# Recurrent mixer: where the casts to the matmul format run, and the low part of the mixed output

## The chip, the cores and the metric

The kernel runs on one core of one Trainium2 chip. The metric is the device time of one execution in microseconds, the median over several runs. The core has a matrix engine (TensorE; PE in the profile, its weight loads PEld), three engines for elementwise work (VectorE is DVE, ScalarE is ACT, GpSimd is POOL) and a queue engine for loads (SyncE, SP). Each engine runs its own instructions strictly in the order in which they stand in its queue; between engines, semaphores hold an instruction until its data are there.

## The reference

A trunk of two layers on 512 tokens of width 1024. Layer 0 has a convolution mixer, layer 1 a recurrent mixer; behind each stands a mixture of 16 experts. The change lies in the recurrent mixer of layer 1:

```python
u = jnp.einsum("bsd,de->bse", x, w_in)
y_branch, xr = jnp.split(u, 2, axis=-1)
xr = causal_depthwise_conv(xr, c_dw) + c_dw_b
...
r = jax.nn.sigmoid(jnp.einsum("bshi,hij->bshj", xh, w_gate_a) + b_gate_a)
i = jax.nn.sigmoid(jnp.einsum("bshi,hij->bshj", xh, w_gate_x) + b_gate_x)
...
a = jnp.exp(log_a)
mult = jnp.sqrt(-jnp.expm1(2.0 * log_a))
b = mult * (i * xr).astype(jnp.float32)
_, h = lax.associative_scan(_linear_recurrence_combine, (a, b), axis=1)
out = jax.nn.gelu(y_branch) * h.astype(x.dtype)
return jnp.einsum("bse,ed->bsd", out, w_out)
```

## The kernel before, in words

Every matrix product that must hold float32 precision is made of three products: each operand is split into a high part (the value cast to the matmul format fp32r) and a low part (the value minus the high part). `hilo` does this for activations: the cast on ScalarE (`act=True`) or on VectorE (`act=False`), the subtraction always on VectorE. The same is done for weights in `Stream`: the cast on ScalarE (L137), the subtraction (L148) on VectorE or GpSimd in turn. Weights are split a few items ahead of their use (`lead` is 1 to 3 here), in the order of use.

The mixer works with channels on the partitions, in 8 blocks of 128 channels by 512 tokens. A written list, `order1`, sets the order: `x0 a0 x1 i0 x2 g0 x3 y0 x4 g1 a1 x5 y1 i1 x6 g2 y2 x7 y3 g3 o y4 o y5 o y6 o y7`. An item `xn` projects block n (24 matmuls), moves it out of PSUM on ScalarE (L994), adds three convolution taps on VectorE (L997) and splits the result into `xch`. `an` and `in` take gate weights. `gn` makes the gates of two blocks: 24 matmuls that read `xch`, four sigmoids and two tanh on ScalarE (L973, L977), products on GpSimd (L978, L984), two roots on ScalarE (L983). `yn` projects the other branch and applies Gelu on ScalarE (L1007). `o` takes a row of output weights.

The recurrence itself is VectorE's: `recurrence` (L925 to L932: an add, two reciprocals, a multiply-add, a product, a scan for each block) is cut into pieces, and after each item `spend` puts as many pieces into VectorE's queue as a budget allows. As soon as block c has both its Gelu branch (`gy`) and its scan (`hv`), `finish(c)` multiplies them (L938) and splits the product into `mixo`, the input of the output projection (L651).

All order is fixed when the program is written: instructions stand in each engine's queue in the order in which these Python lines run. The output projection (`odd_out`) comes after the whole list: for token tiles of 128, first the channel blocks 0 to 3 of all four tiles, then blocks 4 to 7, with the residual sum, the normalisation and the routing behind each tile; then the experts.

Of the kernel before, what the change touches and what calls it, by code (L numbers as in the profile page):

```python
# [11 lines left out]
F32 = mybir.dt.float32  # L12
# [3 lines left out]
AF = mybir.ActivationFunctionType  # L16
OP = mybir.AluOpType
# [330 lines left out]
class Trunk:  # L348
# [564 lines left out]
    def rglru_mixer(self, xT, first, wa, prm, hook):  # L913
        nc, ws, v, lsc = self.nc, self.ws, self.nc.vector, self.lsc
# [21 lines left out]
        def finish(c):  # L936
            y = ys.pop(c)
            v.tensor_tensor(y, y, hs.pop(c), op=OP.mult)  # L938
            m = self.V([P, 2, T], F32R, "mixo")
            self.hilo(m[:, 0], m[:, 1], y, False)  # L940
            self.mixo[c] = m

        credit = [0.0]
# [1 line left out]
        def spend(budget):  # L945
            credit[0] += budget
            while credit[0] > 0:
                c = len(self.mixo)
                if c in ys and c in hs:
                    finish(c)  # L950
                    credit[0] -= 1.3
                elif work:
                    cost = next(work[0], None)
                    if cost is None:
                        work.popleft()
                    else:
                        credit[0] -= cost
                else:
                    credit[0] = 0.0

        def gates(h):
            tp, t1 = [], []
            for i in range(2):
                j = 2 * h + i
                got = []
                for w, bias in ((wg[h // 2][0], B_GA), (wg[h // 2][1], B_GX)):
                    wh, wl = w
                    c0, k0 = i * P, 2 * (h % 2)
                    ps = self.bank()
                    self.mm3(ps, [((wh[:, k0 + q, c0:c0 + P], wl[:, k0 + q, c0:c0 + P]), xch[2 * h + q])  # L970
                                  for q in range(2)])
                    s = self.W([P, T], F32, "gt")
                    nc.scalar.activation(s, ps, AF.Sigmoid, bias=prm[:, j, bias:bias + 1])  # L973
                    got.append(s)


                nc.scalar.activation(got[0], got[0], AF.Tanh, scale=lsc[:, j:j + 1])  # L977
                nc.gpsimd.tensor_tensor(got[1], got[1], xc.pop(j), op=OP.mult)  # L978
                tp.append(got[0])
                t1.append(got[1])  # L980
            for i in range(2):
                s = self.W([P, T], F32, "sq")
                nc.scalar.activation(s, tp[i], AF.Sqrt, scale=4.0)  # L983
                nc.gpsimd.tensor_tensor(t1[i], t1[i], s, op=OP.mult)  # L984
            work.append(recurrence(h, tp, t1))

        self.out_begin(self.korder(1))
        for pos, item in enumerate(self.order1):
            kind, n = item[0], int(item[1:] or 0)
            hook(item)  # L990
            if kind == "x":
                ps = first.pop(0) if first else self.project_in(xT, ws.get())
                x = self.W([P, T], F32, "xc")
                nc.scalar.activation(x, ps, AF.Identity, bias=prm[:, n, B_C:B_C + 1],  # L994
                                     scale=prm[:, n, W_C + 3:W_C + 4])
                for s in range(1, 4):
                    v.scalar_tensor_tensor(x[:, s:], ps[:, 0:T - s], prm[:, n, W_C + 3 - s:W_C + 4 - s],  # L997
                                           x[:, s:], op0=OP.mult, op1=OP.add)
                xc[n] = x
                m = self.V([P, 2, T], F32R, "xch")  # L1000
                self.hilo(m[:, 0], m[:, 1], x, False)
                xch[n] = (m[:, 0], m[:, 1])
                spend(1.5)
            elif kind == "y":
                ps = self.project_in(xT, ws.get())
                y = self.W([P, T], F32, "gy")
                nc.scalar.activation(y, ps, AF.Gelu_apprx_tanh)  # L1007
                ys[n] = y
                spend(4.0)
            elif kind in "ai":  # L1010
                if item != "a0":
                    wg.setdefault(n, []).append(ws.get())
            elif kind == "g":
                gates(n)
                if n % 2:
                    wg.pop(n // 2)
                spend(3.0)
            else:
                self.out_weights(1)
# [783 lines left out]
```

## Time and profile before

| | us |
|---|---|
| median of 3 runs | 1525.57 |
| lowest, highest | 1524.83, 1527.47 |
| the profiled execution, time | 1530.19 |
| the profiled execution, span of its instructions | 1528.4 |

| engine | busy us in the span | share |
|---|---|---|
| TensorE, matmuls | 1396.3 | 91% |
| VectorE | 1126.9 | 74% |
| ScalarE | 772.2 | 51% |
| GpSimd | 432.9 | 28% |

The profile is one execution, taken by the hardware profiler. Its times count from the start of its span. It is read in views: a table of stages (busy time of each engine in a stretch), groups of equal instructions by line, a list of waits (who waited for whom), and timelines of single engines. In a row of a timeline the number in brackets is the engine's idle time ahead of it and the instruction that ended it. Consecutive instructions of an engine overlap a little, so that a duration can be slightly longer than the distance to the next start. Idle time of an engine that nobody waits for costs nothing.

### The profile page before, as it was taken

What the parts mean: (1) busy time and instruction counts of PE and PEld (TensorE: products, weight loads), DVE (VectorE), ACT (ScalarE), POOL (GpSimd) and SP (SyncE); (2) the same over time, 40 slices, a digit from 0 to 9 for tenths busy, and PEclk for the clock granted to TensorE, in tenths of its full rate; (3) what the DMA queues carried; (4) which work ended last, traced back from release to release, by engine and by line L of the source; (5) the groups of instructions that cost most, each with busy time, mean ns of one, the idle gap of its engine ahead of it and who ended that gap; (6) DMA issues with size and microseconds to landing.
All of it is one profiled execution on the core that took longest, in us unless ns stands there. A gap on an engine that the chain in (4) does not pass through costs nothing. (4 is left out here: it accounts for less than half of the span.)

```text
span 1528.4 us, 18167 instructions
## 1 busy us (share of the span) xinstructions
PE 1396.3 (91%) x6456; PEld 1026.4 (67%) x6456; DVE 1126.9 (74%) x1242; ACT 772.2 (51%) x718; POOL 432.9 (28%) x370
## 2 busy tenths in 40 slices
PE   8999959999999999999689798699999999999972
PEld 7877738677586775677577677485776858665851
DVE  6997788668484774478989987885866748554886
ACT  3543227466473755376546421373755747554741
POOL 3983015204202400003384312250051015000043
PEclk9999979999999999999799999799999999999995
DMA  9645748999999999988823258399999999999771
GB/s 282 219 193 193 286 186 310 392 419 417 420 415 413 421 414 420 420 355 330 228 70 93 94 206 318 144 365 406 421 419 420 410 416 421 415 420 419 286 311 55
DMA packets 120837, 490.71 MB, mean 321 GB/s; under 512 B 14078, under 2 KB 53502, under 8 KB 70564
## 3 DMA queue, kind: packets, MB, share of 16 engines
q1 hardware_dynamic: 102240, 437.29, 72.6%
q0 software_dynamic: 11808, 35.28, 5.9%
q10 hardware_dynamic: 6692, 16.91, 3.0%
q8 instruction: 53, 0.87, 0.2%
q14 instruction: 44, 0.36, 0.1%
HBM read 469.50 MB, written 29.62 MB: 327 GB/s over the span
## 5 line engine op out<-in xcount | busy, mean ns | idle before, releaser
L148 DVE TENSOR_TENSOR wl<-raw,wh 128x2048 fp32r<-128x2048 f32 (+2 forms) x310 | 630.1, 2075 | 242.0 <-ACT wh L137 210.4
L137 ACT ACTIVATE wh<-raw 128x2048 fp32r<-128x2048 f32 (+1 forms) x312 | 535.2, 1757 | 110.3 <-PE p L305 27.0
L305 PE MATMUL p<-wh,xe 128*128 128x512 f32 x1344 | 347.6, 396 | 1.0 <-PEq L1439 0.8
L305 PEld LDWEIGHTS p<-wh,xe 128*128 128x128 f32 x1344 | 248.8, 189 | 56.9 <-issue 7.0
L305 PE MATMUL p<-wl,xe 128*128 128x512 f32 x672 | 187.9, 391 | 3.5 <-DVE wl L148 3.5
L1346 POOL DMA_INDIRECT yd<-y,io x30 | 30.8, 1026 | 497.1 <-ACT y L1344 199.3
L305 PEld LDWEIGHTS p<-wl,xe 128*128 128x128 f32 x672 | 126.0, 188 | 32.3 <-DVE wl L148 5.2
L226 PE MATMUL b<-raw,xs 128*64 128x512 f32 x640 | 146.2, 598 | 0.0
L1278 POOL TENSOR_SCALAR S<-c,posp 128x128 bf16<-128x128 bf16 x96 | 127.0, 1337 | 0.5
L596 PE MATMUL b<-xT,wh 128*128 128x512 f32 (+1 forms) x320 | 119.2, 379 | 6.0 <-ACT wh L137 6.0
L597 PE MATMUL b<-xT,wh 128*128 128x512 f32 (+1 forms) x320 | 118.5, 377 | 3.0 <-DVE xT L421 3.0
L1331 POOL DMA_INDIRECT xe<-x1d,ii x32 | 37.3, 1167 | 291.9 <-PE b L271 138.4
L226 PEld LDWEIGHTS b<-raw,xs 128*64 128x64 f32 x640 | 42.4, 136 | 75.0 <-issue 69.6
L148 POOL TENSOR_TENSOR wl<-raw,wh 128x1024 fp32r<-128x1024 f32 x28 | 71.3, 2555 | 29.3 <-ACT wh L137 14.9
L599 PE MATMUL b<-xT,wl 128*128 128x512 f32 (+1 forms) x320 | 73.5, 373 | 3.8 <-DVE wl L148 3.8
L596 PEld LDWEIGHTS b<-xT,wh 128*128 128x128 f32 x320 | 62.3, 195 | 17.7 <-ACT wh L137 7.6
L597 PEld LDWEIGHTS b<-xT,wh 128*128 128x128 f32 x320 | 62.2, 194 | 13.8 <-DVE xT L421 3.6
L226 PE MATMUL b<-raw,hts 128*64 128x512 f32 x320 | 70.9, 595 | 0.0
L599 PEld LDWEIGHTS b<-xT,wl 128*128 128x128 f32 x320 | 56.9, 191 | 14.3 <-DVE wl L148 4.2
L1344 ACT ACTIVATE y<-p,sg 128x512 f32<-128x512 f32 x40 | 25.3, 685 | 75.4 <-PE p L305 75.4
L761 DVE SCALAR_TENSOR_TENSOR b<-av,c,b 128x510 f32<-128x510 f32 (+27 forms) x87 | 59.8, 731 | 2.2 <-ACT b L754 1.3
L326 DVE TENSOR_TENSOR hs<-hs,p 128x512 f32<-128x512 f32 x44 | 30.2, 685 | 39.6 <-PE p L305 39.6
(309 smaller groups left out, 1913.4 us busy)
## 6 DMA issues: line engine op xcount, KB each, us to landing
raw<-in_moe_w_dram SPq DMA_DIRECT2D x384, 1024.0 KB, 15.3
raw<-in_even_w_in_dram SPq DMA_DIRECT2D x20, 512.0 KB, 7.5
yd<-zero ACTq DMA_DIRECT2D x8, 1024.0 KB, 5.0
ay<-yd POOLq DMA_DIRECT2D x8, 1024.0 KB, 15.0
raw<-in_odd_w_in_dram SPq DMA_DIRECT2D x16, 512.0 KB, 7.5
raw<-in_even_w_out_dram SPq DMA_DIRECT2D x8, 512.0 KB, 8.5
x1d<-z POOLq DMA_DIRECT2D x8, 512.0 KB, 7.6
az<-x1d POOLq DMA_DIRECT2D x8, 512.0 KB, 12.2
```

The source lines that it names most:

```text
L137: self.k.nc.scalar.activation(wh, raw, AF.Copy)
L148: self.lo[0].tensor_tensor(wl, raw, wh.bitcast(F32), op=OP.subtract)
L226: self.nc.tensor.matmul(ps[64 * h:64 * h + 64], stat[i], w[0][:, i, h * HALF:(h + 1) * HALF], start=(first and i == 0), stop=(last and i = ...
L305: self.nc.tensor.matmul(pss[j], stat[i][a], q[:, i, j * HALF:(j + 1) * HALF], start=(first and i == 0 and a == 0 and q is wh), stop=(last ...
L326: self.nc.vector.tensor_tensor(self.hm[h], self.hm[h], self.p3[h], op=OP.mult)
L596: nc.tensor.matmul(ps, ah, bh, start=(i == 0), stop=False)
L597: nc.tensor.matmul(ps, ah, bl, start=False, stop=False)
L599: nc.tensor.matmul(ps, al, bh, start=False, stop=(i == n - 1))
L761: nc.vector.scalar_tensor_tensor(o[:, s:], av[:, 0:T - s], prm[:, i, 30 - s:31 - s], acc[:, s:], op0=OP.mult, op1=OP.add)
L1278: (eng or self.nc.vector).tensor_scalar(S[:, t], self.iota2 if small else self.iota, pos[:, t:t + 1], None, op0=OP.is_equal)
L1331: self.nc.gpsimd.indirect_dma_start(out=xe, out_offset=None, in_=self.by_half(self.x1d) if small else self.x1d[:, :], in_offset=bass.Indir ...
L1346: nc.gpsimd.indirect_dma_start(out=self.by_half(self.yd) if small else self.yd[:, :], out_offset=bass.IndirectOffsetOnAxis(ap=slot[2], axi ...
```

## The change

Two places. In `finish`, the cast of the mixed output to its high part goes from VectorE to ScalarE, and the subtraction that makes its low part from VectorE to GpSimd. In the `x` items, `hilo` is called with its default, so that the cast goes to ScalarE; the subtraction stays on VectorE.

```diff
@@ -937,7 +937,8 @@
             y = ys.pop(c)
             v.tensor_tensor(y, y, hs.pop(c), op=OP.mult)
             m = self.V([P, 2, T], F32R, "mixo")
-            self.hilo(m[:, 0], m[:, 1], y, False)
+            nc.scalar.activation(m[:, 0], y, AF.Copy)
+            nc.gpsimd.tensor_tensor(m[:, 1], y, m[:, 0].bitcast(F32), op=OP.subtract)
             self.mixo[c] = m
...
@@ -998,7 +999,7 @@
                                            x[:, s:], op0=OP.mult, op1=OP.add)
                 xc[n] = x
                 m = self.V([P, 2, T], F32R, "xch")
-                self.hilo(m[:, 0], m[:, 1], x, False)
+                self.hilo(m[:, 0], m[:, 1], x)
                 xch[n] = (m[:, 0], m[:, 1])
                 spend(1.5)
```

The new line in `finish` moves all lines below it down by one: L994 before is L995 after.

In ScalarE's queue, at x2 and the gates g0, there stands before (xc is the convolved block as it leaves PSUM, gt are the gates, the number tells buffers apart):

```order
L994 ACTIVATE xc_6312<-b_6287,c_290 128x512
L973 ACT_TABLE_LOAD
L973 ACTIVATE gt_6327<-b_6320,c_290 128x512
L973 ACTIVATE gt_6336<-b_6329,c_290 128x512
L977 ACTIVATE gt_6327<-gt_6327,c_1404 128x512
```

and after:

```order
L995 ACTIVATE xc_6312<-b_6287,c_290 128x512
L418 ACTIVATE xch_6317<-xc_6312 128x512
L974 ACT_TABLE_LOAD
L974 ACTIVATE gt_6327<-b_6320,c_290 128x512
L974 ACTIVATE gt_6336<-b_6329,c_290 128x512
L978 ACTIVATE gt_6327<-gt_6327,c_1404 128x512
```

The cast of x2 now stands between the block's way out of PSUM and the table load of the gates; it reads what VectorE's taps write.

In ScalarE's queue, at the last items y5, y6 and y7, there stands before (gy is the Gelu branch of a block, wh the high part of weights; the second wh_6976 is that of y7, wh_7019 belongs to the output weights):

```order
L1007 ACTIVATE gy_6970<-b_6945 128x512
L137 ACTIVATE wh_6976<-raw_6728 128x1024
L1007 ACTIVATE gy_7005<-b_6980 128x512
L137 ACTIVATE wh_6976<-raw_6728 128x1024
L137 ACTIVATE wh_7019<-raw_6890 128x1024
L1007 ACTIVATE gy_7048<-b_7023 128x512
```

and after:

```order
L1008 ACTIVATE gy_6970<-b_6945 128x512
L940 ACTIVATE mixo_6927<-gy_6970 128x512
L137 ACTIVATE wh_6976<-raw_6728 128x1024
L1008 ACTIVATE gy_7005<-b_6980 128x512
L940 ACTIVATE mixo_7012<-gy_7005 128x512
L137 ACTIVATE wh_6976<-raw_6728 128x1024
L137 ACTIVATE wh_7019<-raw_6890 128x1024
L1008 ACTIVATE gy_7048<-b_7023 128x512
L940 ACTIVATE mixo_7012<-gy_7048 128x512
```

Behind each Gelu stands now the cast of that block's mixed output (c5, c6, c7), which reads what VectorE's product at L938 writes in place; the weight cast of y7 follows the cast for c6.

## Rows read from the trace of the kernel before

**Rows 1.** The table of stages (busy time of each engine in a stretch): stretch in us from the span's start, its length, then TensorE's matmuls busy us (and their count), weight loads, VectorE, ScalarE, GpSimd, granted share of TensorE's clock, mean busy share of the DMA engines, GB/s.

```profile
832.00:863.00 31.00, 22.63 (x99) 18.09 (x97) 30.07 (x37) 14.46 (x18) 9.14 (x5) 0.94 0.21 68
...
863.00:898.00 35.00, 32.97 (x134) 26.19 (x135) 32.96 (x30) 17.88 (x22) 14.52 (x7) 0.95 0.28 97
898.00:947.00 49.00, 48.19 (x247) 40.46 (x246) 33.10 (x53) 5.27 (x8) 4.29 (x6) 1.00 0.81 311
...
947.00:1000.00 53.00, 35.73 (x164) 24.23 (x163) 44.59 (x116) 19.68 (x20) 17.97 (x16) 0.81 0.55 214
1000.00:1490.00 490.00, 475.63 (x2198) 334.94 (x2197) 336.33 (x249) 281.99 (x222) 102.12 (x82) 0.99 0.97 395
```

**Rows 2.** The list of waits of TensorE from 768 to 950 us: who waited for whom, us in total, times, the longest in us.

```profile
PE b L596 <- DVE xch L420: 10.2, 2, 7.7
PE b L599 <- DVE wl L148: 3.8, 1, 3.8
...
PE b L596 <- ACT wh L137: 2.0, 2, 1.7
```

**Rows 3.** The timeline of TensorE's matmuls: start in us, us (of all instructions of the row), engine, line, operation, tiles, shape, count, and in brackets the idle time before it and what ended it. 863.02 is the first matmul of the gates g3, 870.06 the first of the projection behind them (24 matmuls later); 888.88 is the first of y7, 894.46 the first of the output projection (24 matmuls later).

```profile
863.02 0.80 PE L596 MATMUL b<-xch,wh 128*128 128x512 f32 x1 [7.67 <-DVE xch L420]
...
870.06 0.39 PE L596 MATMUL b<-xT,wh 128*128 128x512 f32 x1
...
888.88 0.50 PE L596 MATMUL b<-xT,wh 128*128 128x512 f32 x1 [1.69 <-ACT wh L137]
...
894.46 0.62 PE L651 MATMUL b<-wh,mixo 128*128 128x512 f32 x2
```

**Rows 4.** The groups of instructions from 768 to 912 us, shapes kept apart: line, engine, operation, tiles, shape, count, then busy us in all and mean ns of one, then idle time before them.

```profile
L927 DVE RECIPROCAL gt<-gt 128x256 f32<-128x256 f32 x16 | 27.6, 1739 | 0.3
...
L420 DVE CAST mixo<-gy 128x512 fp32r<-128x512 f32 x8 | 7.6, 946 | 0.4
...
L420 DVE CAST xch<-xc 128x512 fp32r<-128x512 f32 x8 | 6.7, 836 | 0.5
```

**Rows 5.** The timeline of VectorE at the cast of mixo c0, undisturbed, and at the instruction that follows its subtraction.

```profile
806.64 0.43 DVE L420 CAST mixo<-gy 128x512 fp32r<-128x512 f32 x1
...
807.71 0.42 DVE L925 TENSOR_SCALAR gt<-gt 128x512 f32<-128x512 f32 x1
```

**Rows 6.** The timeline of VectorE from 865 to 908 us: the products of Gelu branch and recurrence (L938, for c3, c6 and c7), the low parts of weights (L148), the casts of mixo for c4 and c5 and the first instruction behind the subtraction of each.

```profile
865.28 0.63 DVE L938 TENSOR_TENSOR gy<-gy,hv 128x512 f32<-128x512 f32 x1
...
875.01 2.26 DVE L148 TENSOR_TENSOR wl<-raw,wh 128x1024 fp32r<-128x1024 f32 x1 [0.95 <-ACT wh L137]
...
880.13 2.50 DVE L420 CAST mixo<-gy 128x512 fp32r<-128x512 f32 x1
...
883.28 0.42 DVE L930 TENSOR_SCALAR aa<-gt 128x512 f32<-128x512 f32 x1
...
889.36 2.51 DVE L420 CAST mixo<-gy 128x512 fp32r<-128x512 f32 x1
...
892.52 1.75 DVE L927 RECIPROCAL gt<-gt 128x256 f32<-128x256 f32 x1
...
897.63 0.69 DVE L938 TENSOR_TENSOR gy<-gy,hv 128x512 f32<-128x512 f32 x1
...
906.85 0.69 DVE L938 TENSOR_TENSOR gy<-gy,hv 128x512 f32<-128x512 f32 x1
```

**Rows 7.** The timelines of ScalarE (first row) and VectorE ahead of and in the first x items: a cast of 512 columns from buffer to buffer and the subtraction that waited for it, the three taps of x0, x1 and x2 (L997), two low parts of weights (L148), and the first instruction of the recurrence (L925).

```profile
759.20 0.65 ACT L418 ACTIVATE xT<-xv 128x512 fp32r<-128x512 f32 x1
...
759.88 0.69 DVE L421 TENSOR_TENSOR xT<-xv,xT 128x512 fp32r<-128x512 f32 x1 [0.89 <-ACT xT L418]
...
768.32 2.32 DVE L997 SCALAR_TENSOR_TENSOR xc<-b,c,xc 128x511 f32<-128x511 f32 x3 [3.80 <-ACT xc L994]
...
775.68 2.30 DVE L997 SCALAR_TENSOR_TENSOR xc<-b,c,xc 128x511 f32<-128x511 f32 x3
...
781.45 7.25 DVE L148 TENSOR_TENSOR wl<-raw,wh 128x1024 fp32r<-128x1024 f32 x2
788.62 2.31 DVE L997 SCALAR_TENSOR_TENSOR xc<-b,c,xc 128x511 f32<-128x511 f32 x3
...
792.04 1.52 DVE L925 TENSOR_SCALAR gt<-gt 128x512 f32<-128x512 f32 x1
```

**Rows 8.** The timeline of GpSimd: an add of the layer's input in rows (L1717), a product in the gates (L978), two low parts of weights (L148).

```profile
770.24 2.42 POOL L1717 TENSOR_TENSOR n<-n,g 128x1024 f32<-128x1024 f32 x1
...
871.03 1.29 POOL L978 TENSOR_TENSOR gt<-gt,xc 128x512 f32<-128x512 f32 x1 [0.66 <-ACT gt L973]
...
879.80 2.55 POOL L148 TENSOR_TENSOR wl<-raw,wh 128x1024 fp32r<-128x1024 f32 x1 [0.26 <-ACT wh L137]
888.91 2.68 POOL L148 TENSOR_TENSOR wl<-raw,wh 128x1024 fp32r<-128x1024 f32 x1 [6.56 <-ACT wh L137]
```

**Rows 9.** The timeline of ScalarE in the gates g1: the table load ahead of the sigmoids, and the two roots (L983, two instructions in 1.15 us, 0.58 for one).

```profile
805.89 1.28 ACT L973 ACT_TABLE_LOAD   x1 [0.56 <-PE b L599]
...
812.53 1.15 ACT L983 ACTIVATE sq<-gt 128x512 f32<-128x512 f32 x2
```

**Rows 10.** The timeline of ScalarE at the first sigmoid of g3 and at the two weight casts behind the Gelu of y6: y7's own, then one for a row of the output weights.

```profile
865.44 0.69 ACT L973 ACTIVATE gt<-b,c 128x512 f32<-128x512 f32 x1 [8.54 <-PE b L599]
...
887.78 2.10 ACT L137 ACTIVATE wh<-raw 128x1024 fp32r<-128x1024 f32 x2
```

## The prediction

> **What bounds the kernel now.** I read the stage table first. The recurrent mixer lies between 766 and 898 us, and in it VectorE is the full engine: 30.07 of 31 us from 832 to 863 and 32.96 of 35 us from 863 to 898, while ScalarE and GpSimd are busy for half and less [rows 1]. After it TensorE does the output projection nearly without a gap (48.19 of 49 us from 898 to 947), and the experts' stage follows. What a change in the mixer is worth is therefore read at one point: when TensorE gets into its last unbroken run. The list of TensorE's waits shows what holds it up before that: 10.2 us in two waits for the cast of the convolved channels on VectorE (the longest 7.67 us, ahead of the last gates, g3, at 863.02), 3.8 us for a low part of weights on VectorE, and only 2.0 us for weight casts on ScalarE [rows 2, 3]. The last of these, 1.69 us, stands right before y7, the last input projection. y7 starts at 888.88 us, and from there TensorE runs on into the output projection at 894.46 [rows 3]. So the start of y7 decides, and already now it hangs on a weight cast on ScalarE.
>
> **What the change removes.** VectorE loses 24 instructions. By the groups, the eight casts of xch are 6.7 us and the eight casts of mixo 7.6 us [rows 4]. A cast and a subtraction of mixo together take 1.07 us undisturbed (806.64 to 807.71) [rows 5], but 3.15 and 3.16 us for c4 and c5 (880.13 to 883.28, 889.36 to 892.52) [rows 6]. Of mixo's, 4 x 1.07 + 3.15 + 3.16 = 10.6 us lie before VectorE's product for c6, on which much will hang below.
>
> **What it adds.** ScalarE gets 16 casts, at 0.65 us each by a cast of the same size from buffer to buffer [rows 7]: 10.4 us on an engine that is half idle. As work that costs nothing; their place in the queue is what counts. GpSimd gets eight subtractions at 1.29 us, by a product of the same shape [rows 8].
>
> **The waits at xch.** VectorE's subtraction now waits for a cast that waits for VectorE's third convolution tap. A hop between the engines takes 0.03 us (759.20 + 0.65 against 759.88) [rows 7], so each x leaves VectorE empty for about 0.72 us where it had 0.46 us of undisturbed work. The cast also stands in ScalarE's queue ahead of the gates: in the order shown, the cast of x2 comes before the table load and the sigmoids of g0. From the table load to the end of the first root such a block takes 7.2 us (805.89 to 812.53 + 0.58 in g1) [rows 9], and VectorE's first step of the recurrence overwrites what that root reads. I walk VectorE's queue to it [rows 7, 8]: taps of x0 end at 770.64; 0.72 empty; the subtraction waits for GpSimd's add until 772.66 and ends at 773.35; taps of x1 2.30, then 0.72 and 0.69, end 777.1; two low parts of weights take 2.3 us undisturbed or 7.25 as in their row beside GpSimd's adds; taps of x2 2.31: 781.7 to 786.7. With 0.7 for hop and cast and 7.2 for the block the recurrence starts at 789.6 to 794.6, against 792.04 now. So what VectorE gains up to there it gives back: -2.4 to +2.6; I take 0, near the middle, as most of those adds are still there.
>
> **VectorE's shift at c6's product.** This product ends at 897.63 + 0.69 = 898.32 us now [rows 6]. From the start of the recurrence on, the shift collects these terms:
> - x3 to x7: five casts go, 5 x 0.46 undisturbed; five empty stretches of 0.72 come: +1.3. One of the casts is stalled now, so +0.2 is as near; I take +0.5.
> - mixo c0 to c5: -10.6 if the two stalls of 2.1 us go too, -6.4 if they only move. They lie beside GpSimd's weight low parts at 879.80 and 888.91 [rows 8], which stay, and VectorE's next instruction with two inputs will meet them. I take -6.4.
> - six subtractions on GpSimd in the same stretch: nothing if each falls under a reciprocal, 6 x 1.29 = 7.7 us if each stops VectorE. No row shows which; I take half, +3.9.
> - ScalarE's block for g3 starts only after the cast of mixo c3, which waits for VectorE's product of 865.28 (0.63): at 866.6 us, where the first sigmoid now runs at 865.44 with its table already in [rows 6, 10]. With the table (1.28 of the block) the block and the weight casts behind it come 0 to 2.4 us later, and VectorE waits for one of these casts already (0.95 us ahead of 875.01): I take +1.5.
>
> Sum: 0 + 0.5 - 6.4 + 3.9 + 1.5 = -0.5 us. Ends: -2.4 + 0.2 - 10.6 = -12.8, and 2.6 + 1.3 - 6.4 + 7.7 + 2.4 = +7.6.
>
> The Trainium skill speaks against the third of these terms (page "SBUF — State Buffer", section "Who interferes with whom"): a VectorE instruction with two inputs in SBUF, or in a two-port mode, and a GpSimd instruction that reads SBUF block each other fully, and whoever is first wins. The casts of 2.50 and 2.51 us beside GpSimd's rows at 879.80 and 888.91 agree [rows 6, 8]. Taken to the letter for all six, the term would be the upper end and not its half.
>
> **The decisive edit: mixo's cast on ScalarE.** In the new order ScalarE's queue reads: Gelu of y6, cast of mixo c6, weight cast for y7; before, the weight cast stood right behind the Gelu. The mixo cast waits for VectorE's product for c6, a late piece of the recurrence, and nothing behind it can start. Now the pair of weight casts runs from 887.78 on and TensorE has its part at 888.88 [rows 3, 10]. If VectorE's schedule stayed as it is, y7 would start at 898.32 + 0.03 hop + 0.65 cast + 1.05 weight cast + 0.05 = 900.1 us: +11.2. With VectorE's shift it is 899.6, +10.7. TensorE has nothing else to do meanwhile: y7 and then the projection come in its order. A long wait also costs clock: after the 7.67 us the 24 matmuls of g3 took 7.04 us (863.02 to 870.06), the 24 of y7 5.58 (888.88 to 894.46) [rows 3]: 1.5 us more. Total +12.2.
>
> Hidden, and why: y7's low part (on GpSimd, behind mixo c6's own subtraction, 1.3 + 2.7 us) is needed 16 matmuls, 3.6 us, after y7 starts, so it is about in time. The last mixo (product at 906.85, cast and subtraction 2 us) is needed only when the first four channels of four token tiles are through, 96 matmuls or 22 us after y7; if that cover went, it would cost what it is late.
>
> The experts' stage starts from the routing of what the projection gives, and its loads wait for buffers that this work frees (DMA share 0.55 from 947 to 1000, 0.97 after) [rows 1]; so I carry the delay to the end one for one. The profiled execution has a span of 1528.4 us and a time of 1530.19; the median of the runs is 1525.57, 0.3% less. The difference goes on the median: 1525.57 + 12.2 = 1537.8 us. Its own ends: 11.2 - 12.8 = -1.6 (no clock lost) and 11.2 + 7.6 + 1.5 = +20.3: 1524 to 1546.
>
> **Rivals.**
> - VectorE's relief passes through whole: 6.7 + 10.6 = 17.3 us less on the full engine before c6's product, and nothing new to wait for. y7 then starts at 900.1 - 17.3 = 882.8: -6.1, 1519.5 us. For it: VectorE is 97% busy from 832 to 863, and TensorE's two longest waits are for it. Against: every step above puts ScalarE's queue behind VectorE. It decides only if c6's product ends before 898.32 - 11.2 = 887.1 us.
> - The relief just cancels the hold at y7: VectorE 8 to 13 us ahead at c6, time within 3 us, about 1526. It needs GpSimd's subtractions to fall under reciprocals and both stalls of 2.1 us to vanish.
> - GpSimd's subtractions stop VectorE each time: the third term is 7.7 and not 3.9, 1541.6 us. This is the page's rule at work everywhere. For it: the stalled casts. Against: the 16 reciprocals, 27.6 us of VectorE's time, show a mean of 1.74 and no such stall [rows 4].
> - The change doesn't do what it says, as ScalarE would need table loads for its casts: the two weight casts at 887.78 follow a Gelu and take 2.10 us together, with no room for a load of 1.28 [rows 10], so no.
>
> **How the numbers follow.** My forecast (hold at y7, half of the collisions) 0.66; GpSimd stopping VectorE each time 0.12; cancelled 0.11; relief passing through 0.08; 0.03 for slower than 1546. About 0.2% (3 us) is what a measurement of this kernel can tell from no change. Faster 0.09, within 0.11, slower 0.80. The range for 8 in 10 leaves out the relief case and the far end: 1525 to 1545.
>
> **What would show it.** Right: TensorE waits 8 to 12 us ahead of y7's first matmul, ended by the weight cast on ScalarE, at about 900 us; ScalarE's casts of xch and mixo wait for VectorE; VectorE is empty for 0.7 us ahead of each xch subtraction and for some 3 to 6 us ahead of the first step of the recurrence; the wait ahead of g3 is still 7 us or more. Wrong: y7 before 892 us, TensorE's longest wait elsewhere, or an experts' stage that gives back what the mixer lost.

## The result, and the profile after

The changed kernel takes 1539.12 us (median of 3 runs, 1538.26 to 1539.14) against 1525.57: a ratio of 1.0084, 95% interval 1.0068 to 1.01. It is slower, as forecast (1537.8 us, range 1525 to 1545). Its profiled execution is the 1539.12 one, with a span of 1537.5 us.

The list of waits of TensorE in the mixer (768 to 962 us) answers to [rows 2]: the weight casts on ScalarE stand first now, where they had 2.0 us before.

```profile
PE b L596 <- ACT wh L137: 14.0, 5, 8.6
PE b L596 <- ACT xch L418: 10.5, 3, 8.1
PE b L597 <- DVE xch L421: 2.5, 2, 2.3
```

TensorE's timeline, at the places of [rows 3]: the first matmul of g3, the first of y7, the first of the output projection.

```profile
865.55 0.79 PE L596 MATMUL b<-xch,wh 128*128 128x512 f32 x1 [8.14 <-ACT xch L418]
...
900.40 0.79 PE L596 MATMUL b<-xT,wh 128*128 128x512 f32 x1 [8.55 <-ACT wh L137]
...
908.23 0.62 PE L651 MATMUL b<-wh,mixo 128*128 128x512 f32 x2
```

g3 is 2.5 us later than before, y7 11.5 us, the projection 13.8 us. These are times of two spans, and in this one the mixer begins 2.2 us sooner: counted from a mark ahead of the mixer (see the experiments) they are 4.7, 13.7 and 16.0 us. The table of stages answers to [rows 1]: VectorE is less full, 27.52 of 31 us where it had 30.07 and 30.16 of 35 where it had 32.96, in part because it now waits, and TensorE, which did 32.97 us of matmuls between 863 and 898, does 24.99.

```profile
832.00:863.00 31.00, 24.73 (x109) 19.85 (x107) 27.52 (x31) 19.73 (x25) 15.26 (x9) 0.97 0.11 34
863.00:898.00 35.00, 24.99 (x94) 19.13 (x94) 30.16 (x27) 18.14 (x24) 16.58 (x10) 0.84 0.26 91
```

ScalarE's timeline shows why. First the cast of x2 with the table load and the roots of g0 behind it (its row names no releaser; VectorE's taps of x2 end at 788.66, 0.16 us ahead of it); then the Gelu of y6, the cast of mixo c6, and behind that y7's weight cast (before, it followed the Gelu at 887.78 [rows 10]).

```profile
788.82 0.63 ACT L418 ACTIVATE xch<-xc 128x512 fp32r<-128x512 f32 x1 [9.81 <-issue]
789.47 1.28 ACT L974 ACT_TABLE_LOAD   x1
...
795.73 1.15 ACT L984 ACTIVATE sq<-gt 128x512 f32<-128x512 f32 x2
...
894.11 0.58 ACT L1008 ACTIVATE gy<-b 128x512 f32<-128x512 f32 x1
...
898.77 0.63 ACT L940 ACTIVATE mixo<-gy 128x512 fp32r<-128x512 f32 x1 [4.08 <-DVE gy L938]
899.31 1.99 ACT L137 ACTIVATE wh<-raw 128x1024 fp32r<-128x1024 f32 x2
```

VectorE's timeline: x1's subtraction and the two low parts of weights behind it, the first step of the recurrence, a reciprocal, a scan, a low part that waits for a weight cast behind g3's block, an add of the recurrence, and the product for c6. The product ends at 898.68, where it ended at 898.32 before [rows 6]. The reciprocal and the scan belong to the next fence, the low part and the add to the account of the prediction.

```profile
776.48 2.77 DVE L421 TENSOR_TENSOR xch<-xc,xch 128x512 fp32r<-128x512 f32 x1 [0.76 <-ACT xch L418]
779.17 7.26 DVE L148 TENSOR_TENSOR wl<-raw,wh 128x1024 fp32r<-128x1024 f32 x2
...
796.39 0.43 DVE L925 TENSOR_SCALAR gt<-gt 128x512 f32<-128x512 f32 x1 [6.21 <-ACT sq L984]
...
811.50 1.75 DVE L927 RECIPROCAL gt<-gt 128x256 f32<-128x256 f32 x1
...
838.31 2.20 DVE L932 TENSOR_TENSOR_SCAN hv<-aa,gt 128x512 f32<-128x512 f32 x1
...
878.43 2.26 DVE L148 TENSOR_TENSOR wl<-raw,wh 128x1024 fp32r<-128x1024 f32 x1 [3.14 <-ACT wh L137]
...
886.58 2.56 DVE L925 TENSOR_SCALAR gt<-gt 128x512 f32<-128x512 f32 x1
...
897.99 0.69 DVE L938 TENSOR_TENSOR gy<-gy,hv 128x512 f32<-128x512 f32 x1
```

GpSimd's new subtractions, the first two of eight: the one at 811.88 lies under the reciprocal, which keeps its 1.75; the one at 838.08 began ahead of the scan, which took 2.20 for its usual 1.22.

```profile
811.88 1.30 POOL L941 TENSOR_TENSOR mixo<-gy,mixo 128x512 fp32r<-128x512 f32 x1 [2.62 <-ACT mixo L940]
838.08 1.34 POOL L941 TENSOR_TENSOR mixo<-gy,mixo 128x512 fp32r<-128x512 f32 x1 [1.29 <-PE b L599]
```

### The profile page after: what moved, and what is told of

The parts are those of the page before. It is cut to its first block, busy times and chain, and to the rows that moved or that the text cites. A ratio compares the mean times of both kernels' runs of the same rounds, so it can differ in the third digit from the quotient of the medians.

```text
span 1537.5 us, 18153 instructions
## 1 busy us (share of the span) xinstructions
PE 1398.8 (91%) x6456; PEld 1026.4 (67%) x6456; DVE 1109.1 (72%) x1218; ACT 780.3 (51%) x734; POOL 443.1 (29%) x378
## 5 line engine op out<-in xcount | busy, mean ns | idle before, releaser
L148 DVE TENSOR_TENSOR wl<-raw,wh 128x2048 fp32r<-128x2048 f32 (+2 forms) x310 | 629.8, 2074 | 257.5 <-ACT wh L137 243.0
L226 PE MATMUL b<-raw,xs 128*64 128x512 f32 x640 | 146.2, 598 | 0.0
L596 PE MATMUL b<-xT,wh 128*128 128x512 f32 (+1 forms) x320 | 122.5, 388 | 18.0 <-ACT wh L137 18.0
L597 PE MATMUL b<-xT,wh 128*128 128x512 f32 (+1 forms) x320 | 121.0, 384 | 4.4 <-DVE xT L421 4.4
L596 PEld LDWEIGHTS b<-xT,wh 128*128 128x128 f32 x320 | 64.2, 201 | 31.3 <-ACT wh L137 20.8
L148 POOL TENSOR_TENSOR wl<-raw,wh 128x1024 fp32r<-128x1024 f32 x28 | 71.0, 2544 | 29.6 <-ACT wh L137 14.9
L597 PEld LDWEIGHTS b<-xT,wh 128*128 128x128 f32 x320 | 64.3, 201 | 15.3 <-DVE xT L421 4.8
```

Source lines behind the costliest of these rows:

```text
L148: self.lo[0].tensor_tensor(wl, raw, wh.bitcast(F32), op=OP.subtract)
L226: self.nc.tensor.matmul(ps[64 * h:64 * h + 64], stat[i], w[0][:, i, h * HALF:(h + 1) * HALF], start=(first and i == 0), stop=(last and i = ...
L596: nc.tensor.matmul(ps, ah, bh, start=(i == 0), stop=False)
L597: nc.tensor.matmul(ps, ah, bl, start=False, stop=False)
```

## The experiments

The theory: instructions wait in ScalarE's queue behind casts that wait for VectorE, at y7 above all, and so VectorE's relief cannot be used. Rival A: GpSimd's subtractions stop VectorE, and that is the loss. Rival B: the hand-over at xch is the loss.

Profiles of different executions start the mixer up to 3.7 us apart, so distances are taken from a mark ahead of it that no variant touches, the start of the 16 transposes at L563. In the diffs below, the lines marked with a minus are those of the kernel before (e1, e2, e7, e12, e13) or of the changed kernel (e3, e4, e6). All numbers of the table are us after the mark, read from the timelines; the last column is the ratio to the kernel before on the same chip, with its interval.

| kernel | recurrence starts | c6's product ends | y7 starts | projection starts | ratio |
|---|---|---|---|---|---|
| before | 46.0 | 152.3 | 142.9 | 148.4 | 1 |
| before again (e5) | 46.0 | 152.3 | 142.9 | 148.4 | |
| after | 52.6 | 154.9 | 156.6 | 164.4 | 1.0084 (1.0068 to 1.01) |
| after again (e10) | 50.0 | 152.1 | 153.8 | 161.6 | 1.007 (1.0052 to 1.0088) |
| e1, xch only | 50.1 | 159.1 | 149.6 | 155.2 | 1.0033 (1.0018 to 1.0047) |
| e2, mixo only | 46.2 | 145.2 | 147.0 | 154.7 | 1.0033 (1.0022 to 1.0044) |
| e3, late casts | 50.1 | 152.2 | 145.7 | 151.3 | 1.0007 (0.9994 to 1.002) |
| e4, low part on VectorE | 50.2 | 156.6 | 158.4 | 165.5 | 1.0103 (1.0083 to 1.0122) |
| e6, low part on GpSimd only | 46.2 | 146.6 | 139.4 | 154.5 | 1.004 (1.0025 to 1.0055) |
| e7, x2 on VectorE | 48.9 | 158.5 | 149.0 | 154.6 | 1.0042 (1.0027 to 1.0057) |
| e12, x0 to x2 on VectorE | 46.3 | 156.1 | 146.6 | 152.2 | 1.0034 (1.0021 to 1.0046) |
| e9, mixo only, late | 46.1 | 145.3 | 138.8 | 144.4 | 1.0011 (0.9997 to 1.0024) |
| e11, e9 with rows of its own | 46.3 | 146.2 | 139.7 | 145.3 | 0.9978 (0.9968 to 0.9987) |
| e13, before with rows of its own | 46.2 | 152.4 | 143.0 | 148.6 | 0.9999 (0.9989 to 1.0008) |

**e1: the casts of xch alone.**

```diff
-                self.hilo(m[:, 0], m[:, 1], x, False)
+                self.hilo(m[:, 0], m[:, 1], x)
```

> Only the casts of xch go to ScalarE; mixo is split on VectorE as before. Theory (a queue effect in two places: ScalarE holds y7's weight cast behind mixo's cast, and the subtractions of xch make VectorE start the recurrence 4.4 us late, 796.39 for 792.04): no hold at y7, which follows g3 at the old distance of 25.9 us; but VectorE has the casts of mixo back and the late start, so g3 starts 4 to 8 us after 863.0, and the time is 1530 to 1534. Rival A (GpSimd's subtractions of mixo stop VectorE, and that is the loss): they are gone here, so 1524 to 1527. Rival B (the hand-over at xch is the whole loss): 1537 to 1541.

Measured 1530.03 us. TensorE's timeline, the first matmul of g3 and that of y7:

```profile
868.15 0.80 PE L596 MATMUL b<-xch,wh 128*128 128x512 f32 x1 [11.13 <-ACT xch L418]
...
893.92 0.50 PE L596 MATMUL b<-xT,wh 128*128 128x512 f32 x1 [1.69 <-ACT wh L137]
```

The theory's numbers came: g3 6.9 us later after the mark, y7 25.8 us behind it as before and with its old wait of 1.69 us, so no hold. VectorE's product for c6 is 6.8 us late.

**e2: mixo's part alone.**

```diff
-            self.hilo(m[:, 0], m[:, 1], y, False)
+            nc.scalar.activation(m[:, 0], y, AF.Copy)
+            nc.gpsimd.tensor_tensor(m[:, 1], y, m[:, 0].bitcast(F32), op=OP.subtract)
```

> Only mixo is changed (cast on ScalarE, subtraction on GpSimd); xch is split on VectorE as before. Theory: the recurrence starts at 792 again, 4.4 us or more earlier than with both, c6's product comes at 891 to 895, and y7 waits for it through ScalarE's queue until 893 to 897: a wait of 7 us or more ahead of y7 ended by the weight cast, time 1530 to 1534. Rival A: the GpSimd subtractions are all there, so nearly the whole loss stays, 1537 to 1540. Rival B: 1519 to 1526, as VectorE has relief and nothing to pay.

Measured 1529.81 us. VectorE's product for c6 and TensorE's first matmul of y7:

```profile
888.54 0.69 DVE L938 TENSOR_TENSOR gy<-gy,hv 128x512 f32<-128x512 f32 x1
```

```profile
890.96 0.79 PE L596 MATMUL b<-xT,wh 128*128 128x512 f32 x1 [8.52 <-ACT wh L137]
```

The product comes 7.1 us earlier than before, and yet y7 starts 4.1 us later, 1.73 us after the product's end. In after, e4 and e10 this distance is 1.72, 1.73 and 1.72: the hold. The theory's windows are times of before's span, and this mixer starts 2.0 us sooner: so counted, the product's end (891.3) and y7 (893.0) stand at their lower edges. Against rivals A and B, each part alone costs, and the two add up: c6's product +6.8 and -7.1, with both -0.2 (e10); y7 +6.8 and +4.1, with both +11.0. (In the first profile of after both are some 2.7 us later; see e10.)

**e3: both parts, the mixo casts of c4 to c7 and their subtractions at the end of the list.**

```diff
-            nc.scalar.activation(m[:, 0], y, AF.Copy)
-            nc.gpsimd.tensor_tensor(m[:, 1], y, m[:, 0].bitcast(F32), op=OP.subtract)
+            pend.append((m, y))
+            if c < 4:
+                flush()
...
         spend(1000)
+        flush()
```

(`flush` issues the two removed lines for all that is pending.)

> Both parts of the change, but the casts and subtractions for c4 to c7 are issued at the end of the list of items, behind the Gelu of y7; those of c0 to c3 stand where they stood. No weight cast waits behind them any more; the count of instructions is the same. Theory: y7 follows g3 by 25.9 us as before; with g3 at 863 to 865.5 y7 starts at 889 to 891.5 instead of 900.4, and without the lost clock the time is 1526 to 1529, ten us or more under the changed kernel. Rival A: six of eight subtractions still meet VectorE, or the four late ones meet the sums of the projection: 1535 or more. Rival B: xch is unchanged, so 1537 to 1541.

Measured 1527.36 us. TensorE at y7:

```profile
889.34 0.50 PE L596 MATMUL b<-xT,wh 128*128 128x512 f32 x1 [1.69 <-ACT wh L137]
```

The same instructions, four pairs of them later: y7 is 8.1 us sooner than in e10 and its wait is back to the 1.69 us of before. Most of the loss was the place in the queue, not the work.

**e4: both casts on ScalarE, mixo's low part on VectorE again.**

```diff
-            nc.gpsimd.tensor_tensor(m[:, 1], y, m[:, 0].bitcast(F32), op=OP.subtract)
+            v.tensor_tensor(m[:, 1], y, m[:, 0].bitcast(F32), op=OP.subtract)
```

> Both casts on ScalarE, but the low part of mixo is again VectorE's. Theory: the hold at y7 stays, and VectorE, waiting for each cast and then subtracting (0.7 + 0.6 us for each of six blocks, up to 2 us where GpSimd is in the way), brings c6's product 4 to 8 us later: y7 at 904 to 908, 1542 to 1548. Rival A: six subtractions of 1.27 to 1.34 us no longer stop VectorE, which does them in 0.6: 4 us sooner, 1534 to 1536. Rival B: no change against the changed kernel, 1538 to 1540.

Measured 1541.89 us, 0.1 us under the theory's window; c6's product 4.5 us later than in e10, and the hold at y7 is there again:

```profile
905.32 0.79 PE L596 MATMUL b<-xT,wh 128*128 128x512 f32 x1 [10.02 <-ACT wh L137]
```

Rival A falls as a forecast: with those subtractions off GpSimd the kernel is slower, not faster. As VectorE here also waits for each cast, the run doesn't say what GpSimd's subtractions cost VectorE; that is read from the rows of after.

**e5: the kernel before again.**

> The kernel before once more, unchanged, for a second profile of it. Distances are taken from a mark ahead of the mixer that no variant touches: the start of the 16 transposes at L563 (746.03 us in the first profile). There y7 starts 142.85 us after the mark, the projection 148.43 us, and from the projection to the end of the span are 633.9 us. Theory: y7 is again 142 to 144 us after the mark (its start is set by the order of the queues and not by chance), and the stretch behind the projection is 628 to 630 us as in the five other profiles, so that the first profile's extra 4.6 us lie there and not in the mixer. Rival (the mixer itself differs between executions by several us): y7 more than 2 us off 142.85.

One execution, 1526.17 us. y7 is 142.85 us after the mark in both profiles, and the other places of the table agree within 0.04 us: here the mixer repeats. But from the projection's start to the end of the span are 631.7 us, neither the 633.9 of the first profile nor the 628 to 630 expected. In the kernels that come late it is mostly less (629.3 and 630.0 in the two of after), as if the experts' stage made up some 2 us, but not in all: 631.8 in e12, which is 3.8 us late, and 629.8 in e11, which is early.

**e6: only the low part goes, to GpSimd; both casts on VectorE.**

```diff
-            nc.scalar.activation(m[:, 0], y, AF.Copy)
+            v.tensor_copy(m[:, 0], y)
...
-                self.hilo(m[:, 0], m[:, 1], x)
+                self.hilo(m[:, 0], m[:, 1], x, False)
```

> Only the subtraction of mixo goes to GpSimd; its cast stays on VectorE, and xch is as before, so nothing new stands in ScalarE's queue. Theory (any engine's queue does it): GpSimd's low part of y7's weights now stands behind its subtraction for c6, which waits for VectorE's product and cast of c6. y7 starts on time (within 2 us of 142.9 after the mark), but its 17th matmul waits 5 to 9 us for GpSimd's low part; time 1529 to 1533. Rival A (GpSimd's subtractions cost by stopping VectorE each time): VectorE -0.6 and +1.3 for each, 1528 at the most, with no wait of TensorE for that low part. Rival C (the hold is peculiar to ScalarE): no hold, VectorE relieved by 3.6 us, 1520 to 1523.

Measured 1532.56 us. TensorE at y7, its first and its 17th matmul; then GpSimd's subtraction for c6 and the low part of y7's weights behind it:

```profile
884.18 0.50 PE L596 MATMUL b<-xT,wh 128*128 128x512 f32 x1 [1.69 <-ACT wh L137]
...
895.67 3.78 PE L599 MATMUL b<-xT,wl 128*128 128x512 f32 x8 [7.57 <-POOL wl L148]
```

```profile
891.94 1.38 POOL L941 TENSOR_TENSOR mixo<-gy,mixo 128x512 fp32r<-128x512 f32 x1 [4.94 <-DVE mixo L940]
893.28 2.33 POOL L148 TENSOR_TENSOR wl<-raw,wh 128x1024 fp32r<-128x1024 f32 x1
```

The theory's wait in the expected place: the hold moves to GpSimd's queue, where y7's low part stands behind the subtraction for c6. So it is not peculiar to ScalarE. y7 itself starts at 139.4, 1.5 us sooner than the theory's window.

**e7 and e12: where xch's part loses.** e7 is e1 with x2's cast on VectorE, e12 with those of x0, x1 and x2.

```diff
-                self.hilo(m[:, 0], m[:, 1], x)
+                self.hilo(m[:, 0], m[:, 1], x, n != 2)
```

```diff
-                self.hilo(m[:, 0], m[:, 1], x)
+                self.hilo(m[:, 0], m[:, 1], x, n > 2)
```

> As e1 (xch alone on ScalarE), but the cast of x2 stays on VectorE; the other seven are ScalarE's. Theory (of the 6.8 us that e1 loses up to y7, the greater part is the cast of x2 in ScalarE's queue, which holds the table load and the sigmoids of g0 until VectorE's taps of x2 are through): the recurrence starts 46 to 46.5 us after the mark as before, not 50.1 as in e1, and y7 145 to 147 us after it, not 149.6; time 1525 to 1528. Rival (the loss of e1 is the 0.7 us that VectorE is empty ahead of each of the eight subtractions): y7 at 148.5 to 149.5, time 1529 to 1530.

> As e1 (xch alone on ScalarE), but the casts of x0, x1 and x2 stay on VectorE, so that up to the first recurrence all queues are those of before. Theory (e1's loss has two pieces, 4.1 us up to the start of the recurrence and 2.7 us behind it, at x3 to x7): the recurrence starts 46 us after the mark, y7 145 to 146.5 us after it, ratio 1.001 to 1.0025. Rival D (the whole loss comes from the start, the rest follows from it): y7 at 142.5 to 143.5, ratio 0.9995 to 1.0005. Rival E (VectorE and GpSimd stop each other whatever is gained, as in e7): y7 at 148.5 to 149.6 again, ratio 1.003 to 1.0045.

e7 measured 1532.08 us, e12 1529.87. In e7 the theory fell, and y7, at 149.0, lies in the rival's window. ScalarE's roots of g0 start at 786.09, 41.3 us after the mark against 49.5 in e1, and still the recurrence starts only 1.2 us sooner. VectorE's timeline of e7, and GpSimd's:

```profile
787.78 6.01 DVE L421 TENSOR_TENSOR xch<-xc,xch 128x512 fp32r<-128x512 f32 x1
793.71 0.41 DVE L925 TENSOR_SCALAR gt<-gt 128x512 f32<-128x512 f32 x1
```

```profile
788.19 2.55 POOL L978 TENSOR_TENSOR gt<-gt,xc 128x512 f32<-128x512 f32 x2
790.71 2.53 POOL L984 TENSOR_TENSOR gt<-gt,sq 128x512 f32<-128x512 f32 x2
```

VectorE's subtraction of 0.69 us begins 0.41 us ahead of GpSimd's four gate products, takes 6.01 and ends 0.55 us behind the last of them; why it is stopped although it began first isn't shown. In before (e5) it came 2.5 us later after the mark (789.70, mark at 744.27; here 787.78, mark at 744.83) and fell between GpSimd's two pairs (786.79 for 2.59 us, then 789.78). The wait changes its name and remains; the rival's empty stretches alone (0.7 us each, at x0 and x1) don't make the 2.9 us by which the recurrence starts late here.

In e12 the start is that of before but for 0.3 us, and c6's product is still 3.8 us late. ScalarE's timeline of e12 at x6 and g2, and that of before again:

```profile
846.00 0.63 ACT L418 ACTIVATE xch<-xc 128x512 fp32r<-128x512 f32 x1 [9.30 <-DVE xc L997]
846.65 1.28 ACT L973 ACT_TABLE_LOAD   x1
```

```profile
829.84 0.78 ACT L994 ACTIVATE xc<-b,c 128x512 f32<-128x512 f32 x1 [6.98 <-PE b L599]
830.64 1.28 ACT L973 ACT_TABLE_LOAD   x1
```

The gate block of g2 begins 101.0 us after the mark instead of 86.4, since the cast of x6 waits 9.3 us for VectorE's taps in front of it. GpSimd's first product of g1 comes 72.2 us after it instead of 62.5. So every `g` that follows an `x` is held, not g0 alone. Two pieces of the 3.8 us stand in VectorE's timeline of e12: the first scan takes 3.24 us (1.23 in before), beside a low part of GpSimd's that waited for a weight cast behind x3's cast, and a later step of the recurrence waits 1.60 us for GpSimd's product in the held g1 (no such wait in before).

```profile
803.81 3.24 DVE L932 TENSOR_TENSOR_SCAN hv<-aa,gt 128x512 f32<-128x512 f32 x1
...
819.17 0.43 DVE L930 TENSOR_SCALAR aa<-gt 128x512 f32<-128x512 f32 x1 [1.60 <-POOL gt L978]
```

```profile
803.07 2.90 POOL L148 TENSOR_TENSOR wl<-raw,wh 128x1024 fp32r<-128x1024 f32 x1 [8.43 <-ACT wh L137]
```

y7 (146.6) is 0.1 us beyond the theory's window and some 2 us or more from both rivals', but the ratio lies in the window of rival E and can't be told from that of e1. How the whole 6.8 us of e1 divide between held gates and moved collisions stays open.

**e9: mixo only, the casts and subtractions of c3 to c7 at the end of the list.** As e3 with `c < 3`, and `hilo(..., x, False)` for xch.

> Mixo's part of the change alone (cast on ScalarE, subtraction on GpSimd), with the casts and subtractions of c3 to c7 issued at the end of the list of items, behind the Gelu of y7; xch is split on VectorE as before. Theory: VectorE keeps the relief of e2 (its product for c6 came 7 us sooner than before), and neither g3's block nor y7's weight cast stands behind a mixo cast: g3 at 112 to 113 us after the mark as in e2 (117.2 before), y7 25.7 us later or somewhat less, at 136.5 to 139.5 (142.85 before); time 1520 to 1523.5 or a ratio of 0.996 to 0.998, the first variant under the kernel before. Rival (what the mixer gains is given back in the experts' stage, which waits for its loads): y7 as early, but the ratio 0.999 to 1.001. Rival A: the subtractions of GpSimd eat it, y7 at 142 or later.

Measured 1529.51 us: y7 is 4.1 us ahead, as the theory had it, and the time no better, as the rival had it (its window ends at 1.001, measured 1.0011). TensorE's timeline shows a second wait for gathered rows (an expert's token rows, fetched by an indirect load that GpSimd issues) in the experts' stage, which no profile of before has; GpSimd's gather for it, and VectorE beside that:

```profile
996.93 1.98 PE L271 MATMUL b<-c,xe 128*128 128x128 f32 x8 [4.46 <-DMA xe<-x1d,ii]
```

```profile
986.45 2.96 POOL L1338 DMA_INDIRECT xe<-x1d,ii  x1 [23.81 <-DVE io L1325]
```

```profile
986.22 6.90 DVE L148 TENSOR_TENSOR wl<-raw,wh 128x2048 fp32r<-128x2048 f32 x3
```

In before (e5) this gather was issued 0.08 us ahead of VectorE's low parts and took 1.02 us:

```profile
989.57 1.02 POOL L1331 DMA_INDIRECT xe<-x1d,ii  x1 [22.39 <-PE p L305]
```

```profile
989.65 6.90 DVE L148 TENSOR_TENSOR wl<-raw,wh 128x2048 fp32r<-128x2048 f32 x3
```

**e10: the changed kernel again.**

> The changed kernel once more, for a second profile and an interval from the chip on which e9 runs. In its first profile y7 starts 156.57 us after the mark and the projection 164.40, 13.7 and 16.0 us later than before; 1.4 us of it are older than the change's first instruction (the taps of x0 start 23.70 us after the mark there, 22.3 in all others). Theory: without that, y7 at 154.5 to 156 and the projection 2.2 us more behind than y7, and the time 1.008 to 1.010 of before, since of 15 us at the projection's start some 2 are made up by the experts' stage. Rival (all of the lateness passes to the end): 1.0095 to 1.0105.

Measured 1538.93 us; y7 comes 0.7 us ahead of the window given, the projection is 2.2 us further behind as expected, and the ratio is just under the theory's. The rival (all passes) is out by the ratio. Of the 2.7 us by which y7 was later in the first profile, 2.6 are there when the recurrence starts, and 1.3 already at x0's taps, which wait 5.19 us for ScalarE there and 3.92 here. TensorE's timeline shows where these come from. The second batch of transposes ahead of the mixer, first in the first profile, then in e10:

```profile
748.56 1.86 PE L563 MATMUL b<-c,n 128*128 128x128 f32 x15 [1.06 <-ACT n L1677]
```

```profile
749.81 3.46 PE L563 MATMUL b<-c,n 128*128 128x128 f32 x15 [1.05 <-ACT n L1677]
```

In the first profile this batch ran at a granted clock of 1.00 (2.4 GHz), in e10 at 0.50 (1.2 GHz). Then it turns: x0's matmuls stay at 0.50 until 18.0 us after the mark in the first profile, where in e10 they are at 1.00 by 15.6 us. Of the other profiles only e11 has the fast batch, and its taps too wait longer (4.52 us; 3.8 to 4.0 in the rest). The other 1.3 us arise behind it: x0's and x1's subtractions and the two low parts take 12.9 us in the first profile and 11.6 in e10, as they meet GpSimd's adds at other points. So the mixer does differ between executions by 2.7 us. Why the clock was granted sooner in two profiles isn't shown.

**e11 and e13: rows of its own for the second expert's gather, in e9 and in before.**

```diff
+        mine = rows
+        if layer:
+            mine = self.V([P, D], F32, "xe2")
+            nc.gpsimd.memset(mine, 0.0)
...
-        xe = self.gather(slots[1], 1 in SMALL, rows)
+        xe = self.gather(slots[1], 1 in SMALL, mine)
```

> As e9, and the rows gathered for the second expert of layer 1 go into a buffer of their own, so that this gather waits only for its list of rows and not for TensorE to be through with the first expert's. In e9 it was issued at 986.45 us, 0.23 us behind VectorE's first of three low parts in a row, took 2.96 us and landed 10.4 us later; TensorE waited 4.46 us for it, and the 5.8 us by which the experts had started sooner were gone. Theory (this late gather swallowed the gain): it is issued about 0.8 us sooner, ahead of the low parts, takes 1.0 to 1.1 us, TensorE's second wait for gathered rows is gone, and the time is 0.996 to 0.9985 of before. Rival (the experts' weights are a floor, the DMA engines being full from 1000 us on): the wait is gone too, but the time stays at 0.9995 to 1.0015.

> A control for e11: the kernel before with that buffer of its own for the second expert's rows, the mixer unchanged. There the gather was not late (1.02 us, issued 0.08 us ahead of VectorE's low parts), so both theories expect no change: ratio 0.999 to 1.001, y7 at 142.85.

e11 measured 1520.43 us, e13 1524.68. GpSimd's gather in e11 and VectorE's low parts:

```profile
983.97 1.03 POOL L1338 DMA_INDIRECT xe<-x1d,ii  x1 [21.77 <-DVE io L1322]
```

```profile
983.99 4.51 DVE L148 TENSOR_TENSOR wl<-raw,wh 128x2048 fp32r<-128x2048 f32 x2
```

Issued ahead of the low parts, by 0.02 us only, it takes 1.03 us again; TensorE's second wait is gone and e9's lead reaches the end. The buffer alone changes nothing (e13). e11 is the one version faster than both kernels.

## Why the prediction was right, and where it was not

- **The hold at y7.** Right. The step said 1.78 us from the end of c6's product to y7; four profiles show 1.72 or 1.73. e3 shows that the place does it, e6 that another queue does it too.
- **VectorE's shift at c6's product.** The sum was right, -0.5 against -0.2 us (e10; +2.6 in the first profile), for wrong reasons: two terms were badly sized and cancelled. That the time came out 1.3 us from the forecast is therefore luck in this term. Xch's part was forecast at 0 + 0.5 and is +6.8 (e1), outside its own ends of -2.2 to +3.9; mixo's was -6.4 + 3.9 + 1.5 = -1.0 and is -7.1 (e2), inside its ends.
  - **The start of the recurrence**, "I take 0": 4 us late in e1, e3, e4 and e10, 6.6 in the first profile; the walk's far end was 2.6. The walk let x1's subtraction pass in 0.69 us and chose the middle between 2.3 and 7.25 for the two low parts behind it. In after they took 2.77 and 7.26, beside GpSimd's adds. The block itself was well priced: cast and gates 0.65 + 7.2 = 7.9 forecast, 7.6 from x2's cast to the recurrence (788.82 to 796.39).
  - **x3 to x7**, +0.5: only empty stretches were counted. They are there, 8 times and 6.2 us in all, 0.8 at most, in VectorE's list of waits; but x4's and x6's casts also hold g1 and g2. The walk had seen this at g0 and did not repeat it. It makes 2.7 us by difference in e1, and 3.5 in e12, where these five casts alone are moved.
  - **Six subtractions on GpSimd**, +3.9: in after three lie under reciprocals (811.50, 860.52, 892.51) and cost nothing, three beside scans (838.31, 869.39, 884.47), which take 2.18 to 2.20 for 1.22: 2.9 us. The first of these scans took 2.20 in e5 as well, beside a gate product, so some 1.9 us are new.
  - **Mixo's removal**, -6.4: of the two stalls of 2.1 us one vanishes with its cast and one moves on, to an add that takes 2.56 us for its usual 0.41 (886.58 in after, 877.13 in e2), beside GpSimd's low part at 886.13. That makes some -8.5.
  - **g3's late block**, +1.5: VectorE's wait for the weight cast behind it is 3.14 us in after, 3.0 in e10 and 2.87 in e2, where it was 0.95 [rows 6]: +2, within the term's 0 to 2.4.
  - These three make some -4.6 of e2's -7.1. The other 2.5 us lie between the products for c0 and c4, in other places where VectorE and GpSimd meet; they were not measured one by one.
- **The clock.** 1.5 forecast, 2.2 measured: y7's 24 matmuls take 7.83 us in after (900.40 to 908.23) and 7.75 in e10, 5.58 before. The granted share over these matmuls is 0.69, 0.70 and 1.00. In after they come behind the wait of 8.55 us: up to 904.8 they start some 0.43 us apart, at a share of 0.50 (1.2 GHz), and behind that 0.23.
- **Carried to the end one for one.** Nearly: of 16.0 and 13.2 us at the projection 13.6 and 10.7 arrived (after, e10), of e1's 6.8 some 5.0, of e6's and e7's 6 all. The same step would have failed for a gain: in e9 nothing of 4.1 us arrived.
- **The signs.** Of those named for being right, one is just outside its window: VectorE is empty for 6.21 us ahead of the recurrence, not 3 to 6. The others came, and none of those for being wrong did, but for the 2 us or so given back.
- **The rivals.** "The relief passes whole" had the right source of a gain (e2: -7.1 us at c6) and no way to it as the queues stand; with the casts late and the gather freed, e11 gets 1520.4. "GpSimd stops VectorE each time" is refuted by the reciprocals: beside three of the six subtractions VectorE kept its pace (1.75 us as ever). The rule of the Trainium skill (page "SBUF — State Buffer", section "Who interferes with whom") speaks of VectorE's instructions with two inputs in SBUF or in a two-port mode; taken as it stands, not for all six, it fits: the scans were stopped (2.18 to 2.20 us for 1.22) and the reciprocals, with one input, were not.

## What to carry to other kernels

An instruction that waits for another engine is priced by what stands behind it in its own queue, and not by its length: 0.65 us of cast cost 11 us of start. Put such work behind the last instruction that someone else is waiting for, and repeat the test at every place where the pattern occurs. A sum that comes out right does not vouch for its terms; only a run of each part alone does.

## What was not expected of the hardware

- Which of GpSimd's gather and VectorE's run of two-input subtractions (L148) comes first, by hundredths of a us, goes with how long the gather's issue takes: ahead by 0.02 to 0.10 us it took 1.02 or 1.03 (all profiles but e9's); behind by 0.23 us it took 2.96 in e9 (landing 10.4 us after its issue), and behind by 0.1 us the next gather took 2.09 in e11 (995.24, VectorE at 995.13) and in e13 (1002.89, VectorE at 1002.79). No run changed this order alone, so that the one causes the other is argued and not shown.
- VectorE and GpSimd meet so often in this mixer that taking work from VectorE partly moves the stops: the 6.01 us subtraction of e7.
- The mixer's timing repeated within 0.04 us in the two profiles of before, and differed by 2.7 us in the two of after, where TensorE's granted clock rose at other points ahead of x0's end (e10). The stretch behind it varies by some 2 us.
